# Causal attentions that take two heads at a time, in halves of the tensor engine's array

## The chip, the cores and the metric

The kernel runs on one core of a Trainium2 chip. A core has a tensor engine (PE), which multiplies a stationary operand, loaded into its 128 by 128 array, with a moving one that streams through, and writes to eight PSUM banks of 128 partitions by 512 float32; VectorE (DVE), ScalarE (ACT) and GpSimd (POOL), each with its own queue of instructions; and a DMA queue that SyncE (SP) issues. The metric is the device time of one execution in microseconds, the median of three runs before: 2312.58 us (2312.52 to 2315.58). The profile is that of one further execution.

## The reference

Four layers work on 256 tokens of width 1024 (batch 1), in float32. Layers of the first kind (two) mix four branches, three of which are attentions of 8 heads of width 64; layers of the second kind (two) have one such attention of 4 heads, with width 96 for scores and 64 for values. All four are causal softmax attentions over the 256 tokens:

```python
# fox: decay sums cf of the forget gates enter the scores
logits = jnp.einsum('bqhd,bkhd->bhqk', qb, k).astype(jnp.float32) * scale
logits = logits + cq[..., :, None] - cf[..., None, :]
logits = jnp.where(kpos[None, :] <= qpos[:, None], logits, -jnp.inf)
p = jax.nn.softmax(logits, axis=-1).astype(v.dtype)
return jnp.einsum('bhqk,bkhd->bqhd', p, v)
...
# latent attention, second kind of layer
s = jnp.einsum('bhqd,bhkd->bhqk', q[:, :, start:end], k[:, :, :end]).astype(jnp.float32) * scale
s = jnp.where(qi[:, None] >= ki[None, :], s, -jnp.inf)
p = jax.nn.softmax(s, axis=-1).astype(v.dtype)
outs.append(jnp.einsum('bhqk,bhkd->bhqd', p, v[:, :, :end]))
```

Of moba, whose block is as long as the 256 tokens, plain causal attention is left; dsa masks all but the 64 keys that an index branch scores highest. After the mixer follow gates and projections of the branches, an output product, norms, attention over a memory (second kind) and a feed-forward part.

## The kernel before

**Large products.** Weights stream from memory in chunks of two k tiles by up to 512 columns. ACT rounds a chunk to its high part (`high`, tile `rt<-raw`), DVE subtracts to get the low part (`low`), and PE makes three passes of each product (`mm3`). They are the rows `bank<-rt` of 128x256 or 128x512; 652 chunks of 512 KB feed them, beside some smaller ones. Every other product (`bank<-ft`, plain float32; `bank<-qt`) belongs to the branches.

**Order of the work.** The program is written out once by a planner. It keeps a rough clock of each engine (`Model`, `Engine.cost`) and writes large products one after the other; between them (`tick`) it steps the lanes, generators that write the branches' work piece by piece. A lane's step is written when the planner's clock says that what its last step wrote is done, three PSUM banks are free, and DVE and ACT are not far behind. So the order on each engine is fixed when the program is built; on the chip only semaphores hold an instruction back. The planner prices a float32 product on PE by its stationary and moving widths alone:

```python
one = max(m / 1.2, n / 2.4) + 2
return one if ins[0].dtype == F32R else max(112.0, max(2 * m / 1.2, 4 * n / 2.4))
```

All instructions come from one helper (`call`), so every row of the profile has its line, L362; the tiles tell them apart: `ft` is working memory in float32, `rt` holds rounded operands, `qt` small operands of the decay sums.

**Attention** (`attention`, a lane's generator; lanes A and C in the first kind of layer). One step h does up to three things, for three heads in a software pipeline. Values of head h-2: three products with the transposed probabilities, 128 by 128, as stationary operand and the head's 64 value columns moving. Transposes of head h-1: three of 128 by 128 into a bank, which DVE copies out (`COPY`, 128x384). Scores of head h: q stationary, 64 partitions by 128, against 128 and 256 keys, for fox each after a product that adds the decay sums (`sel`, made by POOL); then DVE adds the mask and takes the minimum (`tensor_tensor_reduce`, the profile's `CUSTOM_DVE_ANT_0`, which is `ISA` in the order), and ACT takes exponentials with their sums. Even heads lie on partitions 0 to 63 and odd ones on 64 to 127. After four heads DVE divides the 128x512 result by the sums, and `attn_out` transposes it (four of 128 by 128) and splits it into high and low part, as the projection needs it. There are 2 x 3 x 8 + 2 x 4 = 56 heads and 14 groups of four.

**Places of other work that the prediction reads.** The index branch of the first kind of layer (`index`) has score products of 64 partitions by 128 and top-8 rounds on DVE. In the second kind of layer the gated branch (`gla`, from L1858) multiplies 32 partitions by 64 columns, in the order that decides what may overlap:

```python
for j in range(2):
    h = 2 * hp + j
    rs = slice(32 * h, 32 * h + 32)
    for q in range(4):
        sl, r = slice(q * 64, (q + 1) * 64), 64 * (q % 2)
        self.mm(bb[j][r:r + 64, q // 2 * 64:q // 2 * 64 + 64], a_[rs, sl], c_[rs, sl])
```

Here `rs` is the row group of the array, `r` its column half (the partitions of the result), and `bb[0]`, `bb[1]` are two banks. The delta branch (`dn`) has products of 128 partitions by 64 columns of 128 moving ones.

Of the kernel before, what the change touches and what calls it, by code (L numbers as in the profile page):

```python
# [14 lines left out]
OP = mybir.AluOpType  # L15
# [44 lines left out]
# branch order in which a mixer's gates and projections are taken  # L60
# [103 lines left out]
class Arena:  # L164
    """Words of a tile, handed out and taken back as the program is written. With aligned set, sizes are
    powers of two and lie at multiples of themselves."""
# [8 lines left out]
    def find(self, free, n):  # L175
        """The offset for n words, or None: the tightest place, the longest unused of these."""
# [95 lines left out]
class Mat:  # L272
    """An operand of the large products in two parts, high and low: [128, a, b] each."""
# [13 lines left out]
class Pair:  # L287
    """Two such operands side by side, of four k tiles each."""
# [16 lines left out]
class Model:  # L305
    """A rough clock of the engines, by which the order of the work is chosen."""
# [45 lines left out]
class Engine:  # L352
    """An engine whose instructions are also put on the model's clock."""
# [37 lines left out]
class Kern:  # L391
    def __init__(self, tc, dram, layers, tiles, due=None):
# [15 lines left out]
        # the stream of weights  # L408
# [87 lines left out]
    def high(self):  # L496
        """High part of the next chunk."""
# [55 lines left out]
    def spawn(self, gen, key=None):  # L553
        """Work in steps that starts now and goes on as its operands come about."""
# [23 lines left out]
    def scoped(self, fn, *args):  # L578
        """Calls fn; returns the time at which all that it wrote is done."""
# [27 lines left out]
    def relieve(self):  # L607
        """Work that may give memory back, ahead of its turn."""
# [22 lines left out]
    def lead(self, name):  # L631
        """How far ahead of its operands a step may be written: nothing where the tensor engine would wait."""
# [25 lines left out]
    def g1(self, out, layer, name, lhs, t, nch, last_use, kt0=0, first=True, last=True, wait=None):  # L658
        """out[token, column] of token tile t over nch chunks of a block; wait(p) sees to the operand of chunk p."""
# [16 lines left out]
    def g11(self, outs, layer, name, lhs, nch, wait):  # L676
        """outs[t][token, column] of both token tiles, chunk by chunk."""
# [14 lines left out]
    def g2(self, outs, layer, name, lhs, cols, nch, last_use=True):  # L692
        """outs[i][channel, token] for column ranges cols of a block."""
# [20 lines left out]
    def head(self, layer, specs, lhs, mid=None):  # L714
        """First blocks after a norm: all of token tile 0, then all of tile 1."""
# [10 lines left out]
    def square_sum(self, f, i, src, eng, scale=1.0):  # L726
        """f[:, i] = sum of squares of scale * src."""
# [7 lines left out]
    def norm_steps(self, t, src, gain, dst, f=None):  # L735
        """Norm of a row tile, into dst() transposed and split; f holds the sums of squares of its halves."""
# [1926 lines left out]
```

## Time and profile before

| what | us |
|---|---|
| median of 3 runs (lowest, highest) | 2312.58 (2312.52, 2315.58) |
| span of the profiled execution | 2314.6 |
| PE busy | 2274.7 (98%) |
| DVE busy | 1509.7 (65%) |
| ACT busy | 1073.3 (46%) |
| POOL busy | 260.7 (11%) |

The profiled execution's own time is its span, 2314.6 us, within the three runs; nothing more of it is given. A busy PE need not be PE at its peak, since matmul spans overlap and their ends are modelled: how long a group of passes takes is read from its start to the start of what follows. The clock that PE was granted is full (1.00) in the mixers of the first kind of layer.

### The profile page before, as it was taken

The page shows a single profiled execution, that of the slowest core. Times are in us where ns is not written, and L with a number is a line of the kernel's source. Part 1 is how long each engine was busy: PE and PEld are TensorE (multiplying, and loading weights), DVE is VectorE, ACT ScalarE, POOL GpSimd, SP SyncE. Part 2 cuts the span into 40 slices and gives each one's busy share as a digit, 9 for nine tenths or more (in the row PEclk, how much of TensorE's full clock was granted, in tenths as well). Part 3 has the DMA queues.
Part 4 walks back from the last instruction along what each step waited for, and adds up shares of the span by engine and source line. Part 5 has one row for each costly group of instructions (what it writes and reads, how often), then busy time and mean ns, then how long its engine had stood idle before and what let it go on. Part 6 is the DMA issues. An engine that isn't in the chain of part 4 may idle for free.

```text
span 2314.6 us, 40370 instructions
## 1 busy us (share of the span) xinstructions
PE 2274.7 (98%) x16412; PEld 2060.1 (89%) x16412; DVE 1509.7 (65%) x2397; ACT 1073.3 (46%) x1691; POOL 260.7 (11%) x244
## 2 busy tenths in 40 slices
PE   8999999999999999999999999999999999999998
PEld 6888998899788899889988899988988889998897
DVE  7777657555877655765578767555556786755554
ACT  4454445444445544544454335444445424544543
POOL 3012020000300302000021320000002132000000
PEclk9999999999999999999999999999999999999999
DMA  6434556655533345565544336456553424645563
GB/s 224 140 116 136 149 180 207 199 173 167 175 126 126 124 157 196 177 234 190 168 128 139 100 119 216 149 172 226 182 165 126 150 84 136 216 146 168 190 202 109
DMA packets 106662, 375.48 MB, mean 162 GB/s; under 512 B 12474, under 2 KB 12908, under 8 KB 106476
## 3 DMA queue, kind: packets, MB, share of 16 engines
q1 hardware_dynamic: 106476, 372.91, 49.3%
q8 instruction: 128, 2.10, 0.4%
q14 instruction: 58, 0.48, 0.1%
HBM read 371.81 MB, written 1.05 MB: 161 GB/s over the span
## 4 chain that ended last, share of the span: by engine, by line
PE 89%; DVE 5%; issue 2%; DMA 1%; ACT 1%; POOL 1%; SPq 0%; POOLq 0%; DVEq 0%; ACTq 0%
PE bank L362 89%; DVE ft L362 3%; DVE rt L362 2%; DMA raw<-in_wts_a 1%; POOL ft L362 1%; ACT rt L362 1%; DMA ft<-in_positions 0%; ACT ft L362 0%; SPq L430 0%; ACT junk L362 0%; DVE junk L362 0%; POOLq L2658 0%; DVEq L362 0%; POOLq L362 0%; ACTq L362 0%
## 5 line engine op out<-in xcount | busy, mean ns | idle before, releaser
L362 PE MATMUL bank<-rt 128*128 128x256 f32 (+2 forms) x12720 | 2001.7, 316 | 13.9 <-DVE rt L362 13.8
L362 PEld LDWEIGHTS bank<-rt 128*128 128x128 f32 x12720 | 1778.7, 191 | 175.1 <-DVE rt L362 19.3
L362 DVE TENSOR_TENSOR rt<-raw,rt 128x1024 fp32r<-128x1024 f32 (+2 forms) x692 | 838.7, 1238 | 343.1 <-ACT rt L362 341.7
L362 ACT ACTIVATE rt<-raw 128x1024 fp32r<-128x1024 f32 (+2 forms) x692 | 698.3, 1034 | 381.2 <-PE bank L362 216.3
L362 POOL TENSOR_TENSOR ft<-ft 128x512 f32<-128x512 f32 (+7 forms) x186 | 211.7, 1146 | 1826.1 <-DVE ft L362 1593.4
L362 PE MATMUL bank<-ft 64*64 64x64 f32 (+10 forms) x3644 | 361.2, 263 | 19.1 <-DVE ft L362 12.3
L362 PEld LDWEIGHTS bank<-ft 128*128 128x128 f32 (+6 forms) x3644 | 288.9, 154 | 67.8 <-DVE ft L362 15.7
L362 ACT ACTIVATE ft<-bank 128x512 f32<-128x512 f32 (+4 forms) x252 | 133.6, 535 | 312.9 <-PE bank L362 274.5
L362 ACT ACTIVATE ft<-ft 128x128 f32<-128x128 f32 (+7 forms) x206 | 88.6, 440 | 229.3 <-DVE ft L362 218.0
L362 DVE SCALAR_TENSOR_TENSOR ft<-ft 128x512 f32<-128x512 f32 (+5 forms) x211 | 94.0, 467 | 41.9 <-ACT junk L362 20.6
L362 DVE TENSOR_TENSOR ft<-ft 128x512 f32<-128x512 f32 (+5 forms) x122 | 69.2, 568 | 65.9 <-ACT ft L362 62.9
L362 DVE SCALAR_TENSOR_TENSOR ft<-bank,ft 128x254 f32<-128x254 f32 (+6 forms) x176 | 80.5, 482 | 31.8 <-ACT ft L362 12.8
L362 ACT ACTIVATE rt<-bank 128x512 fp32r<-128x512 f32 (+1 forms) x102 | 56.0, 554 | 96.2 <-PE bank L362 95.3
L362 DVE TENSOR_TENSOR ft<-ft,bank 64x512 f32<-64x512 f32 (+3 forms) x92 | 59.4, 645 | 36.7 <-PE bank L362 30.3
L362 ACT ACTIVATE ft<-bank,ft 128x256 f32<-128x256 f32 x108 | 47.3, 482 | 72.8 <-PE bank L362 49.9
L362 DVE TENSOR_TENSOR ft<-bank,ft 128x512 f32<-128x512 f32 (+7 forms) x138 | 59.9, 468 | 29.2 <-PE bank L362 18.3
L362 DVE SCALAR_TENSOR_TENSOR ft<-ft,bank 128x512 f32<-128x512 f32 (+1 forms) x106 | 67.4, 642 | 17.0 <-PE bank L362 9.9
L362 DVE COPY ft<-bank 128x384 f32<-128x384 f32 (+6 forms) x96 | 51.9, 543 | 39.7 <-PE bank L362 37.8
L362 ACT ACTIVATE rt<-ft 128x512 fp32r<-128x512 f32 x58 | 36.5, 630 | 60.5 <-DVE ft L362 60.5
L362 POOL TENSOR_SCALAR qt<-qt,ft 64x256 fp32r<-64x256 f32 (+1 forms) x32 | 33.0, 1033 | 190.9 <-PE bank L362 190.7
L362 ACT ACTIVATE junk<-ft 128x512 bf16<-128x512 f32 (+1 forms) x46 | 27.2, 590 | 58.8 <-DVE ft L362 56.2
L362 DVE SCALAR_TENSOR_TENSOR rt<-bank,rt 128x512 fp32r<-128x512 f32 (+1 forms) x72 | 43.4, 612 | 14.3 <-ACT rt L362 14.2
(37 smaller groups left out, 308.3 us busy)
## 6 DMA issues: line engine op xcount, KB each, us to landing
raw<-in_wts_a SPq DMA_DIRECT2D x340, 512.0 KB, 4.3
raw<-in_wts_b SPq DMA_DIRECT2D x312, 512.0 KB, 4.3
raw<-in_wts_b SPq DMA_DIRECT2D x24, 256.0 KB, 2.7
raw<-in_wts_b SPq DMA_DIRECT2D x8, 440.0 KB, 4.2
raw<-in_wts_a SPq DMA_DIRECT2D x8, 340.0 KB, 4.6
ft<-in_mem SPq DMA_DIRECT2D x4, 512.0 KB, 8.2
ft<-in_x SPq DMA_DIRECT2D x2, 512.0 KB, 3.3
ft<-in_norm_mix_pre SPq DMA_DIRECT2D x2, 512.0 KB, 5.5
```

Of the source, the lines that this page charges most:

```text
L362: r = None if self.dry else f(*args, **kw)
```

## The change

`attention` takes two heads (a pair) in each step. Scores: the four products of both heads (eight for fox) are written alternately, even head on the upper 64 rows of the array, odd head on the lower, into two banks. Softmax: the exponentials' sums are inverted at once, four numbers a pair, and DVE multiplies each head's probabilities (128 and 256 columns) ahead of their transposes. Values: the head's 64 value columns are stationary and the transposed probabilities move (256 columns for the first keys, 128 for the second); even heads write to partitions 0 to 63 of the result and odd ones to 64 to 127, so the result comes out transposed. `attn_out` only splits it, from the bank, or from a copy that ACT makes where there is no room yet for the split result. `sel` makes the decay operands of both heads.

```diff
     def attention(self, heads, qk, sel, bias, v, dst, done):
...
+        st, extras = {}, {}
+        ybank, held = None, []
...
+        n = heads // 2
+        tiles = ((0, 128), (128, 384))
+        room = lambda: self.R.fits(128 * heads, 128 * heads)
...
-        for h in range(heads + 2):
...
-                self.mm(yb[:, 0, hh % 4], pt.a[:, 0:128], v(0, hh))
-                self.mm(yb[:, 1, hh % 4], pt.a[:, 128:256], v(0, hh), stop=False)
-                self.mm(yb[:, 1, hh % 4], pt.a[:, 256:384], v(1, hh), start=False)
...
+        for i in range(n + 2):
+            if i >= 2:
+                pr = i - 2
+                pts = st.pop(("pt", pr))
+                if pr % 2 == 0:
+                    ybank = self.bank()
+                o = 256 * (pr % 2)
+                for kt in range(2):
+                    for j, pt in enumerate(pts):
+                        rows = slice(64 * j, 64 * j + 64)
+                        if kt == 0:
+                            self.mm(ybank[rows, o:o + 256], v(0, 2 * pr + j), pt.a[:, 0:256], stop=False)
+                        else:
+                            self.mm(ybank[rows, o + 128:o + 256], v(1, 2 * pr + j), pt.a[:, 256:384], start=False)
+                for pt in pts:
+                    pt.free()
+            if 1 <= i <= n:
+                ps, pts = st.pop(("p", i - 1)), []
+                for p in ps:
+                    b = self.bank()
+                    for c in range(3):
+                        self.tr(b[:, 128 * c:128 * c + 128], p.a[:, 128 * c:128 * c + 128])
+                    pt = F.alloc(384, "pt")
+                    self.copy(pt.a, b[:, :384])
+                    self.fbank(b)
+                    p.free()
+                    pts.append(pt)
+                st[("pt", i - 1)] = pts
+            if i < n:
+                qks = [qk(2 * i + j) for j in range(2)]
+                bb = [self.bank() for _ in range(2)]
+                extra = extras.pop(i) if sel else None
+                if sel and i + 1 < n:
+                    extras[i + 1] = sel(i + 1)
+                for t in range(2):
+                    sl = slice(128 * t, 128 * t + 128)
...
+                        for j in range(2):
+                            f, rr = extra[0][j]
+                            self.mm(bb[j][:, 256 * t:256 * t + 256], f[:, sl], rr, stop=False)
+                    for j in range(2):
+                        q, k = qks[j]
+                        self.mm(bb[j][:, 256 * t:384 * t + 128], q[:, sl], k[:, 0:128 * t + 128], start=extra is None)
...
-                             accum=rsv[:, i, h:h + 1])
+                    extra[1].free()
+                ps, nm = [F.alloc(384, "p") for _ in range(2)], F.alloc(16, "nm")
+                nv = nm.v(4, 2, 2)
+                for j in range(2):
+                    for t, (a, c) in enumerate(tiles):
+                        self.V.tensor_tensor_reduce(out=ps[j].a[:, a:c], in0=bb[j][:, 2 * a:2 * a + c - a], in1=bias[:, a:c],
+                                                    scale=1.0, scalar=3e38, op0=OP.add, op1=OP.min,
+                                                    accum_out=nv[:, 0, j, t:t + 1])
+                    self.fbank(bb[j])
+                    for t, (a, c) in enumerate(tiles):
+                        self.act(ps[j].a[:, a:c], ps[j].a[:, a:c], AF.Exp, scale=-1.0, bias=nv[:, 0, j, t:t + 1],
+                                 accum=nv[:, 1, j, t:t + 1])
+                self.V.reciprocal(nm.a[:, 8:12], nm.a[:, 4:8])
+                for j in range(2):
+                    for t, (a, c) in enumerate(tiles):
+                        self.ts(ps[j].a[:, a:c], ps[j].a[:, a:c], nv[:, 2, j, t:t + 1], OP.mult)
...
-                self.V.reciprocal(ri.v(2, 4), rsv[:, :, 4 * g:4 * g + 4])
-                self.tt(y.v(8, 64), view(ybank[0], 8, 64), ri.a[:, :, None].to_broadcast([128, 8, 64]), OP.mult)
...
+                st[("p", i)] = ps
+            if i >= 2 and pr % 2 == 1:
+                y, yb, ybank = None, ybank, None
+                if not (m or room()):
+                    y = F.alloc(512, "y")
+                    self.act(y.a, yb)
+                    self.fbank(yb)
+                    held.append((y, pr // 2))
+                else:
+                    m = m or Mat(self, heads // 2, 256, "yT")
+                    self.spawn(self.attn_out(m, None, yb, pr // 2), key)
+            elif held and (m or room()):
...
+                for y, g in held:
+                    self.spawn(self.attn_out(m, y, y.a, g), key)
+                held = []
+            yield
+        while not m and not room():
...
+        for y, g in held:
+            self.spawn(self.attn_out(m, y, y.a, g), key)
...
-    def attn_out(self, m, y, g):
...
-                self.tr(b[:, 256 * c + 128 * t:256 * c + 128 * t + 128], yv[:, t, c])
...
+    def attn_out(self, m, y, src, g):
+        yield from self.split(m, (slice(None), slice(2 * g, 2 * g + 2), slice(None)), view(src, 2, 256))
+        if y is None:
+            self.fbank(src)
+        else:
+            y.free()
...
-            def sel(h):
-                r = slice(64 * (h % 2), 64 * (h % 2) + 64)
-                f = lsel(8 + h, r, 256)
-                return f.a[r], st["rr"].a[r], f
+            def sel(i):
+                f, ops = self.Q.alloc(256, "lsel"), []
+                for j in range(2):
+                    r = slice(64 * j, 64 * j + 64)
+                    c = 8 + 2 * i + j
+                    self.ts(f.a[r], f32(st["base"].a)[r], self.sel[r, c:c + 1], OP.mult, eng=self.P)
+                    ops.append((f.a[r], st["rr"].a[r]))
+                return ops, f
```

On PE, fox in the first layer: a step of before holds values (`128x64 x3`), transposes and scores of one head each (`qt` and `ft` into one bank), then large products (`rt`).

```order
L362 MATMUL bank_74<-ft 128x64 x3
L362 MATMUL bank_68<-ft 128x128 x3
L362 MATMUL bank_70<-qt 128x256
L362 MATMUL bank_70<-ft 128x128
L362 MATMUL bank_70<-qt 128x256
L362 MATMUL bank_70<-ft 128x256
L362 MATMUL bank_75<-rt 128x256 x30
```

And a step of after, at the same place of the program.

```order
L362 MATMUL bank_71<-ft 64x256 x2
L362 MATMUL bank_71<-ft 64x128 x2
L362 MATMUL bank_72<-ft 128x128 x3
L362 MATMUL bank_73<-ft 128x128 x3
L362 MATMUL bank_69<-qt 128x256
L362 MATMUL bank_68<-qt 128x256
L362 MATMUL bank_69<-ft 128x128
L362 MATMUL bank_68<-ft 128x128
L362 MATMUL bank_69<-qt 128x256
L362 MATMUL bank_68<-qt 128x256
L362 MATMUL bank_69<-ft 128x256
L362 MATMUL bank_68<-ft 128x256
```

A step now has the values of two heads (partitions 64, rows `64x256` and `64x128`), six transposes, and scores that alternate between two banks; the large products behind it are not shown.

On DVE, moba in the first layer: of before, the copy of transposes, the two reductions of a head with the reads of their results, and, once in four heads, the reciprocal and the division of the result.

```order
L362 COPY ft<-bank_70 128x384
L362 ISA ft<-bank_69,ft 128x128
L362 ISA ft 128x1
L362 ISA ft<-bank_69,ft 128x256
L362 ISA ft 128x1
L362 RECIPROCAL ft<-ft 128x8
L362 TENSOR_TENSOR ft<-bank_72,ft 128x512
L362 MAX ft<-ft 128x8
```

And of after, from the reductions of a pair's second head on.

```order
L362 ISA ft<-bank_70,ft 128x128
L362 ISA ft 128x1
L362 ISA ft<-bank_70,ft 128x256
L362 ISA ft 128x1
L362 RECIPROCAL ft<-ft 128x4
L362 TENSOR_SCALAR ft<-ft 128x128
L362 TENSOR_SCALAR ft<-ft 128x256
L362 TENSOR_SCALAR ft<-ft 128x128
L362 TENSOR_SCALAR ft<-ft 128x256
L362 TENSOR_TENSOR rt<-raw,rt 128x1024 x2
L362 MAX ft<-ft 128x8
```

The reciprocal now stands in each pair directly behind the reductions, with the four multiplications; weight halves (`rt<-raw`) and the index branch come behind them.

## Rows read from the trace of the kernel before

**Rows 1.** The page's head and its busy line.
```profile
span 2314.6 us, 40370 instructions
...
PE 2274.7 (98%) x16412; PEld 2060.1 (89%) x16412; DVE 1509.7 (65%) x2397; ACT 1073.3 (46%) x1691; POOL 260.7 (11%) x244
```
**Rows 2.** The chain of waits: start, length, engine and tile.
```profile
37.03 349.70 PE bank L362 x2424
...
615.78 342.81 PE bank L362 x2395
```
**Rows 3.** Busy time by engine, sum of 55:115, 115:180 and 180:285.
```profile
sum 230.00, PE 230.00 PEld 203.28 DVE 160.62 ACT 113.42 POOL 26.67; mean PE 76.67 PEld 67.76 DVE 53.54 ACT 37.81 POOL 8.89
```
**Rows 4.** Groups by shape, DVE, 55:285: busy us, mean ns | idle before, releaser.
```profile
L362 DVE TENSOR_TENSOR rt<-raw,rt 128x1024 fp32r<-128x1024 f32 x60 | 75.5, 1273 | 12.0 <-ACT rt L362 12.0
...
L362 DVE CUSTOM_DVE_ANT_0 ft<-bank,ft 128x128 f32<-128x128 f32 x24 | 6.9, 289 | 12.0 <-PE bank L362 11.9
```
**Rows 5.** Who PE waited for: us in total, times, longest.
```profile
PE bank L362 <- DVE rt L362: 13.8, 16, 2.8
PE bank L362 <- DVE ft L362: 12.3, 6, 7.6
```
**Rows 6.** Timeline of a moba head, PE and its loads: start us, us, instruction.
```profile
88.36 1.96 PE L362 MATMUL bank<-ft 128*128 128x64 f32 x13
89.40 0.52 PEld L362 LDWEIGHTS bank<-ft 64*128 64x128 f32 x4 [0.17 <-issue]
90.25 2.94 PEld L362 LDWEIGHTS bank<-rt 128*128 128x128 f32 x24 [0.33 <-issue]
```
**Rows 7.** Timeline of a fox head, and of a step without scores, PE.
```profile
145.36 1.11 PE L362 MATMUL bank<-ft 128*128 128x64 f32 x9
146.39 0.38 PE L362 MATMUL bank<-qt 64*128 64x256 f32 x1
...
147.48 0.74 PE L362 MATMUL bank<-rt 128*128 128x256 f32 x4
...
164.92 1.11 PE L362 MATMUL bank<-ft 128*128 128x64 f32 x9
165.79 2.31 PE L362 MATMUL bank<-rt 128*128 128x512 f32 x9
```
**Rows 8.** Timeline of passes in half of the array, PE (index, delta branch).
```profile
50.02 0.71 PE L362 MATMUL bank<-ft 64*128 64x128 f32 x4
...
58.34 1.13 PE L362 MATMUL bank<-ft 64*128 64x256 f32 x4
...
1360.03 0.65 PE L362 MATMUL bank<-ft 128*64 128x128 f32 x4
1360.61 0.62 PE L362 MATMUL bank<-rt 128*128 128x256 f32 x3
```
**Rows 9.** Timeline of products in quarters and eighths, PE (gated branch).
```profile
1331.06 0.47 PE L362 MATMUL bank<-ft 32*64 32x64 f32 x16
1331.46 0.74 PE L362 MATMUL bank<-rt 128*128 128x256 f32 x4
```
**Rows 10.** Groups by shape, DVE, the whole span: multiplications by a column.
```profile
L362 DVE TENSOR_SCALAR ft<-ft 128x256 f32<-128x256 f32 x30 | 10.5, 371 | 2.3 <-ACT ft L362 1.7
...
L362 DVE TENSOR_SCALAR ft<-ft 128x128 f32<-128x128 f32 x3 | 0.8, 267 | 2.5 <-ACT ft L362 2.4
```
**Rows 11.** Timeline behind the scores of the moba head above, DVE and ACT.
```profile
90.47 0.29 DVE L362 CUSTOM_DVE_ANT_0 ft<-bank,ft 128x128 f32<-128x128 f32 x1 [0.40 <-PE bank L362]
...
90.80 0.40 ACT L362 ACTIVATE ft<-ft 128x128 f32<-128x128 f32 x1 [3.27 <-DVE ft L362]
91.03 0.08 DVE L362 DVE_READ_ACCUMULATOR2_ANT ft<- 128x1 f32 x1
...
91.84 0.20 DVE L362 RECIPROCAL ft<-ft 128x8 f32<-128x8 f32 x1 [0.73 <-ACT ft L362]
92.08 0.69 DVE L362 TENSOR_TENSOR ft<-bank,ft 128x512 f32<-128x512 f32 x1
```

More of the change, by code (lines that the diff above doesn't have):

```diff
@@ L861, in attention @@
         m = None
-        rs = F.alloc(2 * heads + 8, "rs")
-        rsv = rs.v(2, heads)
-        st = {}
-        ybank, ydone, held = [None], None, []
+        st, extras = {}, {}
+        ybank, held = None, []
         key = ("y", id(dst))
-        extras = {}
+        n = heads // 2
+        tiles = ((0, 128), (128, 384))
+        room = lambda: self.R.fits(128 * heads, 128 * heads)
         if sel:
@@ L870, in attention @@
             yield
-        for h in range(heads + 2):
-            if h >= 2:
-                hh = h - 2
-                pt = st.pop(("pt", hh))
-                if hh % 4 == 0:
-                    ybank[0] = self.bank()
-                yb = view(ybank[0], 2, 4, 64)
-                self.mm(yb[:, 0, hh % 4], pt.a[:, 0:128], v(0, hh))
-                self.mm(yb[:, 1, hh % 4], pt.a[:, 128:256], v(0, hh), stop=False)
-                self.mm(yb[:, 1, hh % 4], pt.a[:, 256:384], v(1, hh), start=False)
-                pt.free()
-            if 1 <= h <= heads:
-                p = st.pop(("p", h - 1))
-                b = self.bank()
-                for i in range(3):
-                    self.tr(b[:, 128 * i:128 * i + 128], p.a[:, 128 * i:128 * i + 128])
-                pt = F.alloc(384, "pt")
-                self.copy(pt.a, b[:, :384])
-                self.fbank(b)
-                p.free()
-                st[("pt", h - 1)] = pt
-            if h < heads:
-                q, k = qk(h)
-                b = self.bank()
-                extra = extras.pop(h) if sel else None
-                if sel and h + 1 < heads:
-                    extras[h + 1] = sel(h + 1)
-                for i in range(2):
-                    sl = slice(128 * i, 128 * i + 128)
-                    if extra:
-                        self.mm(b[:, 256 * i:256 * i + 256], extra[0][:, sl], extra[1], stop=False)
-                    self.mm(b[:, 256 * i:384 * i + 128], q[:, sl], k[:, 0:128 * i + 128], start=extra is None)
-                if extra:
-                    extra[2].free()
-                p = F.alloc(384, "p")
-                nm = F.alloc(8, "nm")
-                for i, (a, c) in enumerate(((0, 128), (128, 384))):
-                    self.V.tensor_tensor_reduce(out=p.a[:, a:c], in0=b[:, 2 * a:2 * a + c - a], in1=bias[:, a:c],
-                                                scale=1.0, scalar=3e38, op0=OP.add, op1=OP.min, accum_out=nm.a[:, i:i + 1])
-                self.fbank(b)
-                for i, (a, c) in enumerate(((0, 128), (128, 384))):
-                    self.act(p.a[:, a:c], p.a[:, a:c], AF.Exp, scale=-1.0, bias=nm.a[:, i:i + 1],
-                             accum=rsv[:, i, h:h + 1])
-                nm.free()
-                st[("p", h)] = p
-            if h >= 2 and (h - 2) % 4 == 3:
-                g = (h - 2) // 4
-                ri = F.alloc(8, "ri")
-                y = F.alloc(512, "y")
-                self.V.reciprocal(ri.v(2, 4), rsv[:, :, 4 * g:4 * g + 4])
-                self.tt(y.v(8, 64), view(ybank[0], 8, 64), ri.a[:, :, None].to_broadcast([128, 8, 64]), OP.mult)
-                self.fbank(ybank[0])
-                ri.free()
-                if ydone:
-                    held.append(ydone)
-                ydone = (y, g)
-            elif h >= 2 and ydone and (m or self.R.fits(128 * heads, 128 * heads)):
@@ L928, in attention @@
                 m = m or Mat(self, heads // 2, 256, "yT")
-                self.spawn(self.attn_out(m, *ydone), key)
-                ydone = None
+                for y, g in held:
+                    self.spawn(self.attn_out(m, y, y.a, g), key)
+                held = []
             yield
-        rs.free()
-        while not m and not self.R.fits(128 * heads, 128 * heads):
+        while not m and not room():
             yield
         m = m or Mat(self, heads // 2, 256, "yT")
-        for a in held + [ydone]:
-            self.spawn(self.attn_out(m, *a), key)
+        for y, g in held:
+            self.spawn(self.attn_out(m, y, y.a, g), key)
@@ L941, in attention @@
         done()
-    def attn_out(self, m, y, g):
-        b = self.bank()
-        yv = y.v(2, 2, 128)
-        for c in range(2):
-            for t in range(2):
-                self.tr(b[:, 256 * c + 128 * t:256 * c + 128 * t + 128], yv[:, t, c])
-        yield from self.split(m, (slice(None), slice(2 * g, 2 * g + 2), slice(None)), view(b, 2, 256))
-        self.fbank(b)
-        y.free()
+    def attn_out(self, m, y, src, g):
[4 more added lines that the diff above has]
+            y.free()
     def rope(self, b, nh, t, dup=False):
```

## The prediction

> **What bounds the kernel now.** I read the busy shares first: the tensor engine (PE) stands at 98%, VectorE (DVE) at 65%, ScalarE (ACT) at 46% [rows 1]. A busy PE is not yet a bound, since matmul spans overlap, so the chain of waits comes next: one piece of it is 349.70 us of PE without a break, from 37 to 387 us, which is the whole mixer of the first layer with its three attentions; the second layer has its like [rows 2]. In such a stretch time taken from PE is time taken from the span, until another engine is late. The next view is therefore what DVE does there: in 55 to 285 us, where the 24 heads of layer one lie, it is busy 160.6 of 230 us [rows 3], and its idle time is mostly the time in which it stands ahead of PE: 12.0 us for ACT's half of the next weight chunk and 12.0 us before the first read of the scores are the largest pieces [rows 4]. PE waits for DVE 13.8 + 12.3 us in the whole program [rows 5]. So PE bounds, and DVE has about 69 us to give per layer of the first kind.
>
> **Prices on PE.** A product of float32 operands runs as two passes, each a row of the trace. One moba head: the step starts at 88.36, its scores at 89.40 (the first weight load of 64 rows), the large products go on at 90.25; so 1.04 us for values and transposes and 0.85 us for scores [rows 6]. A fox head takes 1.03 and 1.09 us [rows 7]. The step at 164.92, which has no scores, takes 0.87 us for 6 value passes and 3 transposes, 0.097 us each; with scores behind them the same nine take 0.16 to 0.17 us more, which is the way into 64 rows [rows 6, 7]. In half of the array, four passes of 256 columns take 1.13 us and four of 128 take 0.71, so 128 columns cost 0.105 us and 256 cost 0.21; four of 128 columns in a column half take 0.58 us to the next large product, 0.16 over 4 x 0.105, which is the switch in and out [rows 8].
>
> Do halves run beside each other? The row that bears on it is a score step of the gated branch: 16 passes of 32 rows by 64 columns, which alternate between column halves and go from one row group to the next with the head, end after 0.40 us [rows 9]. A 64-column pass is half of 0.105, so 0.052 us. One after the other they would take 16 x 0.052 + 0.16 = 1.0 us, two at a time 0.58, four at a time 0.37. Measured is 0.40: both row groups and column halves overlap. What no row shows is the width that is used here, 64 rows by 128 columns and 128 rows by 64 with 256 moving; I take the same.
>
> [...]
>
> **The change, part by part (PE).**
> Values: before, 6 passes a head at 0.097, so 1.16 us for two heads. Now 4 passes of 256 and 4 of 128, two at a time: 2 x 0.21 + 2 x 0.105 = 0.63, plus 0.16 for the switch and up to 0.17 for the way in: 0.96. Saved 0.20 us a pair, 28 pairs: 5.6 us.
> Scores: before, each head pays its own stay in 64 rows, 0.85 + 0.17 = 1.02 us (moba, dsa), 1.09 + 0.16 = 1.25 (fox). Now two heads share one stay, in two banks. Saved 1.02 x 16 pairs + 1.25 x 8 pairs = 16.3 + 10.0 = 26.3 us. The four pairs of latent attention have 96 rows and save nothing here.
> Transposes of probabilities: as many as before. Transposes of the result: 4 for each of 14 groups go, 56 x 0.097 = 5.4 us.
> Sum 5.6 + 26.3 + 5.4 = 37 us of PE.
>
> **The change on the other engines.** DVE gains four multiplications a pair, 2 x (0.371 + 0.267) = 1.28 us [rows 10], and a reciprocal of 0.20 [rows 11]. That reciprocal stands right behind the four reductions of both heads and waits for the last exponential, with all of DVE's queue behind it: weight halves, copies for the next step, convolutions. Where a reciprocal now follows one head's exponentials it waited 0.73 us. For two heads: ACT starts 0.33 us after the first reduction and needs 1.04 a head (90.80 to 91.84), so 2.41 us; DVE is busy with reductions for 2 x 0.64 = 1.28 of it (90.47 to 91.11 a head); the wait is 1.1 us [rows 11]. What goes is the division of the result per group, 0.69 + 0.20 + 0.73 = 1.6 us, 0.8 a pair. Net 1.28 + 0.20 + 1.1 - 0.8 = 1.8 us a pair: 21 us in the 12 pairs of a layer, 50 us in all. Layer one's DVE then has 160.6 + 21 = 182 us of queue in 230 - 18 = 212 us of PE (the 18 being half of 37), 86%. So most of it lies in idle time; ACT gains only four copies of a result that finds no room yet, and POOL's work for fox is the same.
> Bounds of what DVE takes back: 0, if the idle time takes all; 50 us, if every pair pays all on the path. The planner (which prices a product in half the array as if it ran alone, and reciprocals and multiplications below their rows) places the next step by its own clock, and between two moba steps stand 48 to 54 large passes, some 6 us, against a chain of reductions, exponentials and multiplications of 1.3 + 1.1 + 1.5 = 3.9 us behind the scores. That fits with 2 us to spare, less whatever stands in DVE's queue ahead. Nearest is the row in which PE waits for DVE only 26 us in the whole program while DVE is idle 69 in one mixer, so I take a fifth, 10 us.
> The rest of the program is planned anew behind each of these steps; PE's waits for DVE there, 26.1 us [rows 5], can move by a few us either way.
>
> **Sum.** The profiled execution had a span of 2314.6 us [rows 1], 2.0 above the median 2312.6 of the three runs, so nothing measurable lies around it. 2314.6 - 37 + 10 = 2287.6 by the span, 2286 by the median. Likeliest case by itself: 2275 (DVE takes nothing back) to 2296 (20 us, twice what I take).
>
> **Rivals.**
> DVE becomes the bound in the mixers (slower than before at its end). Place: the reciprocal behind the exponentials. For it: 86% in a queue that is kept in order, and moba shares its stretch with the top-8 rounds of the index branch. Against: DVE stands ahead of PE in the rows above. With half of the 50 us on the path: 2312.6 - 37 + 25 = 2301. With all of it: 2326. It decides from 37 / 28 = 1.3 us a pair.
> [...]
> Row halves take turns, since each pass fills all 128 output partitions. Of the 26.3 us then stays one way in per pair, 24 x 0.17 = 4: 2286 + 22 = 2308, no change that can be told.
> DVE takes nothing, and in the new order a quarter of the 26.1 us that PE waits for DVE goes too: 2275.6 - 6.5 = 2269.
>
> **How the numbers follow.** About 0.2% (4.6 us) is what a measurement of this kernel can tell from no change. Forecast 2286 (2275 to 2296): 0.62. DVE with half, 2301: 0.12. DVE with all or more, 2317 and above: 0.06. Column halves in turn, 2304: 0.07. Row halves in turn, 2308: 0.05. Below 2275: 0.08. The range that leaves out two in ten: 2267 to 2306. Faster (under 2308): the forecast, the lower case, half DVE and columns, 0.89; within 0.2%: 0.05; slower: 0.06.
>
> **What would show it.** Values right: in each pair 8 rows of 128 x 64 with starts in twos, some 0.8 us to the first transpose; in turn, 1.4. Scores right: the first score to the next large product about 0.9 us for two moba heads and 1.1 for two fox heads; 1.6 or more if rows take turns. DVE right: reciprocals of 4 columns x28 with about 1.1 us idle before each, put down to ACT, and 70% busy turned into some 80% in the mixers; PE's waits for DVE up by about 10 us. The forecast is wrong if large products in 55 to 285 us show gaps before the transposes that wait for DVE by more than 1.3 us a pair, or if the mixer's unbroken PE piece does not shorten by 13 to 18 us.

## The result, and the profile after

The changed kernel takes 2298.95 us (median of 4 runs, 2296.01 to 2300.51), the kernel before 2312.55 us (4 runs on the same chip, 2308.87 to 2315.58). The ratio is 0.9938, its 95% interval 0.9922 to 0.9953: 13.6 us faster, about half of the 26 us forecast. The profiled execution is the fastest of the four runs, and that of before, a further one, is slower than all four of its kernel (a run's time is 1.8 us above its span wherever both are given, which makes it about 2316.4), so the two traces differ by more than the medians: 2314.6 - 2294.2 = 20.4 us of span.

The page of the changed kernel, its head and its busy line:

```profile
span 2294.2 us, 40097 instructions
...
PE 2237.2 (98%) x16244; PEld 2020.1 (88%) x16244; DVE 1526.5 (67%) x2509; ACT 1074.2 (47%) x1695; POOL 271.2 (12%) x244
```

PE still reads 98%, as before [rows 1]: that number hides the loss. The chain of waits shows it in the second layer, whose mixer was one piece of 342.81 us [rows 2] and now lies in several, the longest of them:

```profile
609.01 48.96 PE bank L362 x326
...
695.62 35.68 PE bank L362 x227
...
742.26 59.18 PE bank L362 x377
...
806.12 141.63 PE bank L362 x1092
```

Of the first layer's mixer it shows nothing: followed back from its end, this chain reaches only to 587 us. What ends PE's waits:

```profile
PE bank L362 <- DVE rt L362: 27.7, 20, 3.1
PE bank L362 <- DVE ft L362: 12.0, 6, 7.4
...
PE bank L362 <- POOL qt L362: 3.4, 2, 1.7
```

The wait for `rt` from DVE, which is the low halves of weights, has doubled from 13.8 us [rows 5]; the wait for `ft` is as it was; the one for `qt`, an operand of the state branch made on POOL, is new. The three windows of the first layer's heads, engines in the order PE, PEld, DVE, ACT, POOL, then granted clock, busy share of DMA and GB/s:

```profile
55.00:115.00 60.00, 60.00 (x418) 50.80 (x418) 46.83 (x135) 31.61 (x66) 7.92 (x5) 1.00 0.44 141
115.00:180.00 65.00, 60.16 (x380) 50.56 (x379) 56.53 (x120) 32.86 (x67) 9.56 (x7) 0.95 0.44 137
180.00:285.00 105.00, 101.89 (x755) 92.86 (x754) 67.34 (x132) 50.52 (x98) 17.38 (x13) 1.00 0.46 145
sum 230.00, PE 222.05 PEld 194.22 DVE 170.70 ACT 114.98 POOL 34.86; mean PE 74.02 PEld 64.74 DVE 56.90 ACT 38.33 POOL 11.62
```

PE was busy 230.00 of 230 [rows 3]; now 8 us of the stretch are idle, while DVE stands at 74%. DVE is not full, and PE waits for it: the average does not say what stands ahead of what. The first of the layer's three holes, in a timeline of DVE and PE (start, length, instruction):

```profile
121.92 1.39 DVE L362 TENSOR_TENSOR rt<-raw,rt 128x1024 fp32r<-128x1024 f32 x1
...
121.96 3.86 PE L362 MATMUL bank<-rt 128*128 128x256 f32 x30
123.23 1.01 DVE L362 COPY ft<-bank 128x384 f32<-128x384 f32 x2
...
124.17 0.28 DVE L362 CUSTOM_DVE_ANT_0 ft<-bank,ft 128x128 f32<-128x128 f32 x1
...
126.44 0.18 DVE L362 RECIPROCAL ft<-ft 128x4 f32<-128x4 f32 x1 [1.09 <-ACT ft L362]
126.66 1.01 DVE L362 TENSOR_SCALAR ft<-ft 128x128 f32<-128x128 f32 x4
...
127.58 2.36 DVE L362 TENSOR_TENSOR rt<-raw,rt 128x1024 fp32r<-128x1024 f32 x2
...
128.85 2.36 PE L362 MATMUL bank<-rt 128*128 128x256 f32 x10 [3.03 <-DVE rt L362]
```

A low half ends at 123.3; the next starts at 127.58, 4.3 us later, behind two copies, the four reductions, 1.09 us of waiting, a reciprocal and four multiplications, and takes 1.2. PE's products last until 125.8, 2.5 us from 123.3. It is 4.3 + 1.2 - 2.5 = 3.0 us short, and that is its wait, 3.03. What follows the hole (same columns as the windows above):

```profile
126.00:129.00 3.00, 0.15 (x1) 0.15 (x2) 2.52 (x7) 2.78 (x6) 0.00 (x0) 1.00 0.09 34
129.00:131.00 2.00, 1.88 (x10) 1.64 (x11) 1.93 (x4) 0.00 (x0) 0.00 (x0) 0.66 0.56 109
131.00:133.00 2.00, 2.00 (x11) 1.78 (x12) 1.93 (x5) 0.00 (x0) 0.00 (x0) 0.50 0.93 356
133.00:135.00 2.00, 2.00 (x22) 1.51 (x24) 1.89 (x5) 0.00 (x0) 0.00 (x0) 0.98 0.17 68
```

The granted clock falls to 0.66 and 0.50 in the two windows after the hole, which costs 2 x 0.34 + 2 x 0.50 = 1.7 us more. (That is an estimate: it takes PE's work to go with the clock.) The other two holes of the layer end here:

```profile
176.46 0.38 PE L362 MATMUL bank<-qt 32*128 32x256 f32 x1 [1.68 <-POOL qt L362]
...
240.25 0.98 PE L362 MATMUL bank<-rt 128*128 128x256 f32 x6 [3.11 <-DVE rt L362]
```

The third is of the first one's kind, a wait for a low half. The second is not: there PE waits 1.68 us for `qt` from POOL, and the clock falls too (0.64 from 176.40 to 180.00). The sister layer has the same three, 3.04, 1.70 and 3.10 us.

### The profile page after: what moved, and what is told of

The parts are those of the page before. It is cut to its first block, busy times and chain, and to the rows that moved or that the text cites. A ratio compares the mean times of both kernels' runs of the same rounds, so it can differ in the third digit from the quotient of the medians.

```text
span 2294.2 us, 40097 instructions
## 1 busy us (share of the span) xinstructions
PE 2237.2 (98%) x16244; PEld 2020.1 (88%) x16244; DVE 1526.5 (67%) x2509; ACT 1074.2 (47%) x1695; POOL 271.2 (12%) x244
## 4 chain that ended last, share of the span: by engine, by line
PE 63%; DVE 6%; issue 2%; ACT 1%; DMA 1%; POOL 1%; SPq 0%; POOLq 0%; DVEq 0%; ACTq 0%
PE bank L362 63%; DVE ft L362 4%; DVE rt L362 2%; POOL ft L362 1%; ACT rt L362 1%; ACT ft L362 0%; DMA raw<-in_wts_a 0%; DMA raw<-in_wts_b 0%; DMA ft<-in_positions 0%; POOL qt L362 0%; ACT junk L362 0%; SPq L430 0%; DVE junk L362 0%; POOLq L2676 0%; DVEq L362 0%
## 5 line engine op out<-in xcount | busy, mean ns | idle before, releaser
L362 PE MATMUL bank<-rt 128*128 128x256 f32 (+2 forms) x12720 | 1993.5, 316 | 28.0 <-DVE rt L362 27.7
L362 PE MATMUL bank<-ft 64*64 64x64 f32 (+11 forms) x3476 | 315.6, 266 | 18.8 <-DVE ft L362 12.0
L362 PEld LDWEIGHTS bank<-ft 64*64 64x64 f32 (+6 forms) x3476 | 243.7, 147 | 74.5 <-issue 16.0
L362 ACT ACTIVATE ft<-bank 128x512 f32<-128x512 f32 (+5 forms) x256 | 135.7, 536 | 317.6 <-PE bank L362 290.2
L362 DVE TENSOR_SCALAR ft<-ft 128x256 f32<-128x256 f32 (+7 forms) x236 | 55.4, 277 | 21.3 <-ACT ft L362 9.8
L362 DVE TENSOR_TENSOR ft<-bank,ft 128x512 f32<-128x512 f32 (+8 forms) x124 | 50.3, 442 | 16.1 <-PE bank L362 7.5
L362 POOL TENSOR_SCALAR qt<-qt,ft 64x256 fp32r<-64x256 f32 (+1 forms) x32 | 42.1, 1318 | 131.4 <-PE bank L362 130.5
L362 ACT ACTIVATE junk<-ft 128x512 bf16<-128x512 f32 (+1 forms) x46 | 27.2, 591 | 58.1 <-DVE ft L362 55.6
```

Of the source, the lines that this page charges most:

```text
L362: r = None if self.dry else f(*args, **kw)
```

## A view that the experiments need

All kernels here run the same 12720 large products in the same order. So the start of the n-th of them in each trace, against before, says where time comes and goes; a median only gives the sum. Differences in us, worked out from the traces; positions are behind the attentions of the mixers (first kind, first kind, second, second) and the end:

```
large product        1920    5040    7680   10800   12719
before, us          364.2   915.9  1391.4  1970.5  2307.1
after                -7.4   -10.6   -16.7   -20.1   -20.1
e1 no division      -18.9   -36.5   -37.9   -40.0   -40.1
e2 no mult.         -16.0   -33.1   -29.3   -22.6   -22.6
e3 own step         -16.0   -33.2   -25.9   -23.8   -23.7
e4 price             +1.3    +0.2    +5.4   +18.1   +18.1
e5 own step, first  -18.3   -35.4   -40.3   -39.3   -39.2
e8 plan of after    -13.1   -25.4   -34.3   -37.6   -37.6
e11 latent only      +2.5    +2.5    -2.4    -5.6    -5.6
e12 low earlier     -11.7   -25.5   -31.3   -32.4   -32.2
```

Counted from the span's start, the rows come out up to 0.5 us lower. Up to 2.5 us of a row (3.9 in e12) are there already at product 200, ahead of the first heads. Behind 5040 a row also holds the granted clock of two single executions, and that differs between executions of one kernel: of the runs of before beside e5, one of 2308.23 us had a mean of 0.997 and one of 2318.01 us had 0.992. In the trace of before the clock is 1.00 up to product 5280; its mean is 0.981 from there to 7680 and 0.988 from 7680 to 10800.

## The experiments

Each stood beside runs of before on the same chip; ratios are against those.

**e1: no division.**
```diff
-                self.V.reciprocal(nm.a[:, 8:12], nm.a[:, 4:8])
-                for j in range(2):
-                    for t, (a, c) in enumerate(tiles):
-                        self.ts(..., nv[:, 2, j, t:t + 1], OP.mult)
```


> Leaves out the reciprocals and the multiplications of the probabilities, so the result is not divided; all products stay as in the changed kernel. In the changed kernel the tensor engine's branch products take 34 us less than before, and its large products 14 us more, most of it in gaps of 3 us in which it waits for the low halves of weights. Theory A (the block of reciprocal, its wait of 1.1 us and 1.0 us of multiplications stands in VectorE's queue between two low halves): the gaps go, 14 us come back, 2285 us. Theory B (the gaps come from where the planner puts the low halves, whatever stands in the queue): within 4 us of the changed kernel, 2295 to 2303.

2273.08 us, 0.9825 (0.9812 to 0.9838): 26 us under the changed kernel, where theory A had 14. Theory B's time is out as well, but this run can't separate the two, since without the division the planner also chooses other places (e8 can). In the first two mixers e1 is 18.9 and 36.5 us ahead of before: the whole saving on PE that the prediction worked out for them, 18 us each. The 26 us between e1 and after there (36.5 - 10.6) are the price of the division.

**e2: the multiplications left out, the reciprocal kept.**
```diff
                 self.V.reciprocal(nm.a[:, 8:12], nm.a[:, 4:8])
-                for j in range(2): ...   # the four multiplications
```


> Keeps the reciprocal and its wait for the exponentials, leaves out the four multiplications (the result is not divided). If the wait in the queue costs (1.2 of the block's 2.3 us with the reciprocal itself), half of what leaving out all gives: about 2292 us. If the multiplications as work cost, nearly all of it: 2286. If neither: 2295 to 2303.

2295.1 us, 0.9922 (0.9909 to 0.9936). The median alone would say that the multiplications cost 4 us. The table says otherwise: in the first two mixers e2 is 33.1 us ahead, 22.5 us better than after; the second kind's mixers then lose 10.5 us, where after gained 9.5, with a new order of their own in which the missing multiplications, of 4 latent pairs, can't cost anything. With 1 us less in each block most holes close (up to product 5040 PE waits 12.4 us, 26.1 in after), although the reciprocals wait as before (30.0 us in all). So neither the wait nor the work has a price of its own here. What fits is that their sum uses up a small stock of low halves, which e12 tests.

**e3: reciprocal and multiplications as a step of their own.**
```diff
+                yield
                 self.V.reciprocal(nm.a[:, 8:12], nm.a[:, 4:8])
```


> The reciprocal and the multiplications become a step of their own, which the planner writes when the exponentials are done by its clock; the work is the same. If the wait of 1.1 us in VectorE's queue is what makes low halves late: the idle time before the reciprocals falls from 30.3 us in all to under 10 and the time to about 2290 us. If the work costs and not the wait: the idle time falls too, the time stays at 2295 to 2303. If probabilities come later to their transposes by this: slower, 2305.

2292.66 us, 0.991 (0.9897 to 0.9924). The reciprocals' idle time falls from 30.3 us to nothing, and the first two mixers get 22.6 of the 25.9 us back (33.2 against 10.6), with all the work still there. Again the second kind loses, 9.4 us, by 10800.

**e4: the planner's price of half-array products halved.**
```diff
-            return one if ... else max(112.0, max(2 * m / 1.2, 4 * n / 2.4))
+            return one if ... else self.part * max(112.0, max(2 * m / 1.2, 4 * n / 2.4))
```
(`self.part` is 0.5 around the values, and around scores of 64 rows.)

> Only the planner's price changes: the products of values and scores that run two at a time are priced at half. By its own clock a fox pair takes 3.0 us for values and scores where the trace has 2.0 with the transposes' share taken off, so it believes the tensor engine to be later than it is and writes low halves late. If that makes the gaps: two or more of the six gaps of 3 us go, and the time falls to 2286 to 2292 us. If the order of the queue alone makes them: 2295 to 2303.

2334.19 us, 1.0088 (1.0072 to 1.0103): slower than before, by 21 us. My sign was wrong. The planner writes a low half that is not due yet when DVE's clock is no more than 1500 ns ahead of PE's; a PE clock that runs late lets it write low halves early. The truer price takes that cover away:

```profile
PE bank L363 <- DVE rt L363: 34.4, 30, 4.0
PE bank L363 <- DVE ft L363: 22.9, 15, 7.3
```

PE waits 34.4 us for low halves instead of 27.7 and 22.9 us for `ft` instead of 12.0, and the whole gain of the first two mixers is gone (+0.2 at 5040). These 17.6 us are less than half of the 38.2 by which the span is longer than that of after, and the loss goes on in the second kind (+18.1 at 10800), so the lost cover is the likely cause, argued and not shown; that the price alone moves the time the wrong way is measured.

**e5: e3 in the first kind alone.**
```diff
+                if qks[0][0].shape[0] == 64:
+                    yield
                 self.V.reciprocal(nm.a[:, 8:12], nm.a[:, 4:8])
```


> The reciprocal and the multiplications are a step of their own in the two layers of the first kind alone; the latent attentions of the second kind keep them behind the reductions. With the step of its own everywhere, the first kind's two mixers came 33 us earlier at the same large product than in the kernel before, and the second kind's mixers lost 9 us; the changed kernel's second kind won 10. If the first is due to the step and the second to a new order in layers where the step brings nothing, both gains now add: 2313 - 33 - 10 = 2270 us, 2266 to 2280 with what the new order may do. If the second kind's loss follows from the state in which the first kind leaves the queues: 2290 to 2295 again.

2276.88 us, 0.9836 (0.9816 to 0.9856), with the division whole: it beats both kernels, the changed one by about 22 us. The place of the hole above, in e5:

```profile
120.28 7.94 PE L362 MATMUL bank<-rt 128*128 128x256 f32 x64
120.40 1.01 DVE L362 COPY ft<-bank 128x384 f32<-128x384 f32 x2
121.33 0.28 DVE L362 CUSTOM_DVE_ANT_0 ft<-bank,ft 128x128 f32<-128x128 f32 x1
...
122.44 0.08 DVE L362 DVE_READ_ACCUMULATOR2_ANT ft<- 128x1 f32 x1
122.44 1.22 DVE L362 TENSOR_TENSOR rt<-raw,rt 128x1024 fp32r<-128x1024 f32 x1
```

The low half stands right behind the last reduction, in the time in which DVE used to wait for the exponentials. PE runs 64 products instead of 30 and a hole. The windows' sum over the same 230 us:

```profile
sum 230.00, PE 229.31 PEld 202.38 DVE 178.89 ACT 121.82 POOL 35.38; mean PE 76.44 PEld 67.46 DVE 59.63 ACT 40.61 POOL 11.79
```

DVE is busier than in the changed kernel (178.89 against 170.70 us) and PE is full again. The two gains did not add as expected: the second kind gives 3.8 us here (35.4 to 39.2), not 10; the time came out within the range because the first kind gave 35.4 and not 33.

**e6 and e7: one head's passes written behind the other's,** from e1, the planner's clock fed as before (the edit in outline).
```diff
-                for t in range(2):
-                    for j in range(2):
+                for j in range(2):
+                    for t in range(2):
```
(e6 in the scores; e7 the same with `kt` in the values.)

> From the kernel without reciprocals and multiplications (2273 us, the tensor engine bound): the scores of one head are written behind those of the other instead of in turns, with the planner's clock fed as before, so that nothing else changes its place. The result is not divided. If the two row halves work beside each other, and only where passes of both are next to each other: 16 pairs lose 0.5 us and 8 pairs 0.9 us, less one pass of overlap each, 8 to 15 us: 2281 to 2288. If the gain came from the shared stay in 64 rows alone: within 3 us of 2273.

> The same with the values: both products of one head are written before those of the other; the scores stay in turns. The result is not divided. If the column halves work beside each other: a pair's passes cost up to 4 x 0.21 + 4 x 0.105 instead of half of it, 0.63 us less the overlap of one pass, 28 pairs, 12 to 18 us: 2285 to 2291. If they take turns anyway: 2273.

2276.52 us (0.9831, 0.9811 to 0.9851) and 2272.38 us (0.9816, 0.9798 to 0.9834): neither differs from e1 by what can be told. They did not decide what they were meant to, since for values and for the scores of moba and dsa the written order is not the order of the starts. In e6 the passes of two heads still start 13 ns apart, and two moba heads' scores take 0.86 us (65.96 to 66.82), as in e1 (65.98 to 66.84). In e7 a pair's eight passes still start in twos, 13 and 14 ns apart (7 ns in e1), the four of 256 columns ahead of the four of 128, and take what they took, 94.83 to 95.63:

```profile
94.83 0.88 PE L465 MATMUL bank<-ft 128*64 128x256 f32 x8
95.63 1.57 PE L362 MATMUL bank<-rt 128*128 128x256 f32 x11
```

For fox the order did count. There six passes of one head stand ahead of six of the other, and a pair's scores take 1.42 us in e6 (111.19 to 112.62) instead of 1.09 in e1 (111.19 to 112.28), in all eight pairs, 2.7 us in sum:

```profile
111.19 0.38 PE L465 MATMUL bank<-qt 64*128 64x256 f32 x1
...
112.62 2.66 PE L362 MATMUL bank<-rt 128*128 128x256 f32 x20
```
```profile
111.19 0.39 PE L362 MATMUL bank<-qt 64*128 64x256 f32 x2
...
112.28 2.90 PE L362 MATMUL bank<-rt 128*128 128x256 f32 x22
```

**e8: e1 with the order of the changed kernel** (the edit in outline).
```diff
+                dry, self.V.dry = self.V.dry, True    # counted by the planner, not issued
                 self.V.reciprocal(...)                # and the four multiplications
+                self.V.dry = dry
```


> The changed kernel with its own plan, word for word the same order on all engines, but the reciprocals and multiplications are left out of VectorE's queue (the planner's clock still counts them; the result is not divided). Leaving them out of the plan too gave 2273 us. If the block in the queue makes the low halves late: the six gaps of 1.9 to 3.3 us in the first kind's mixers go and the time is 2270 to 2280. If the planner's places make them: the gaps stay, 2293 to 2301.

2280.69 us, 0.9853 (0.9829 to 0.9878). With every other instruction in its place 14.8 of the 25.9 us come back in the first two mixers (25.4 against 10.6); the other 11 are places that the planner chose because it counts the division, such as the wait for `qt`, which stays at 1.69 us. So queue and plan share the price, in these traces about four to three up to product 5040; at the end e8 and e1 differ by only 2.5 us.

**e9 and e10: both heads in one half of the array,** from e1 with its plan (in outline; fox's decay operands go with the scores, and e10 also writes one head behind the other, which cost nothing in e7).
```diff
-                        q, k = qks[j]
+                        q, k = qks[0] if heads == 8 else qks[j]
```
```diff
-                        rows = slice(64 * j, 64 * j + 64)
+                        rows = slice(0, 64)
```


> From the kernel without reciprocals and multiplications (2273 us), with its plan: the scores of a pair are both computed from the first head's operands, so all passes lie in the same 64 rows; number, size, banks and order stay. What is computed for the second head of a pair is wrong. Writing the heads behind one another cost nothing (2276.5 +- 3), and in its trace the passes of the two heads still start 13 ns apart, so the order doesn't decide; the place does. If row halves work beside each other: 16 pairs lose 0.52 us (2 x 0.21 + 2 x 0.105 less the overlap) and 8 pairs about 0.95, in all 15 to 18 us: 2288 to 2291. If halves are no help: 2273.

> From the same kernel, with its plan: the values of both heads of a pair go through the same 64 columns (into the same rows of the result, so half of it is lost). If column halves work beside each other: 28 x 0.63 = 17.6 us more, 2288 to 2292. If they took turns before too: 2273.

2289.91 us (0.9887, 0.9872 to 0.9903) and 2290.13 us (0.9894, 0.9881 to 0.9908): 16.8 and 17.1 us over e1, as expected. (e1 ran on another chip; by the ratios it is 14 and 16 us, and PE's branch products, idle time taken off, take 16.9 and 17.9 us more in the traces.) A pair's values in one half, and a moba pair's scores in one half:

```profile
98.63 1.51 PE L465 MATMUL bank<-ft 128*64 128x256 f32 x8
100.07 10.20 PE L362 MATMUL bank<-rt 128*128 128x256 f32 x52
```
```profile
66.89 1.57 PE L465 MATMUL bank<-ft 64*128 64x128 f32 x8
68.39 4.58 PE L362 MATMUL bank<-rt 128*128 128x256 f32 x36
```

And the same two in e1:

```profile
65.98 0.93 PE L362 MATMUL bank<-ft 64*128 64x128 f32 x8
66.84 4.58 PE L362 MATMUL bank<-rt 128*128 128x256 f32 x36
...
95.01 0.87 PE L362 MATMUL bank<-ft 128*64 128x256 f32 x8
95.81 6.75 PE L362 MATMUL bank<-rt 128*128 128x256 f32 x37
```

1.44 us instead of 0.80 for the values, 1.50 instead of 0.86 for the scores, and 1.97 instead of 1.09 for fox. So in e1 both kinds of halves work beside each other.

**e11: the latent attentions alone** (in outline).
```diff
-            yield from self.attention(4, ...)     # kernel before
+            yield from self.attention2(4, ...)    # the changed function, here alone
```


> The kernel before, with the change in the four latent pairs of the second kind alone. On the tensor engine these save 0.2 + 0.2 us a pair, 1.6 us in all. In the changed kernel the two second-kind mixers came 9.6 us earlier than before at the same large product. If that is the change's own effect there: 2313 - 10 = 2303, 2301 to 2306. If it came from the state in which the mixers of the first kind leave queues and plan, or from chance in the new order: another number, anywhere from 2305 to 2320.

2309.35 us, 0.9976 (0.9967 to 0.9985): 5.2 us by the median, 8.1 in the trace from 5040 to the end (+2.5 to -5.6). So the change is worth something in these layers by itself, about 5 us, more than the 1.6 of PE work. The larger number of the traces is in part the granted clock: between products 5280 and 10800 it takes 15.3 us from before, 10.2 from e11 and 8.5 from after (what is missing to 1.00, summed), which is 5.1 of e11's 8.1 us and 6.8 of the 9.5 of after (10.6 to 20.1). PE's waits do not explain it: behind product 5280 they are 17.0 us in e11 and 17.4 before. In e2 and e3 they are 27.2 and 28.6, so the next order may lose as much.

**e12: low halves earlier.**
```diff
+        if self.chunks[min(self.i_cur, len(self.chunks) - 1)][0][0] == "a":
+            idle += 1500.0
```


> The changed kernel; in the layers of the first kind the planner may write a low half when VectorE's clock is up to 3000 instead of 1500 ns ahead of the tensor engine's. The work is the same. If the gaps come from too few low halves in stock when the block of a pair stands in the queue: the gaps of 3.2 us go, 14 to 25 us come back: 2274 to 2285. If the stock cannot grow (buffers, or the high halves of ACT): 2295 to 2303. If earlier low halves push scores' reductions back: slower than 2303.

2283.82 us, 0.9867 (0.9853 to 0.988), 15 us under the changed kernel with the same work. The reciprocals still wait (30.0 us), and 14.9 of the 25.9 us come back in the first two mixers. The same allowance holds for ACT's high halves, which may come earlier too. Halves in stock cover the block, as the step of its own moves it; e4 acts on the same condition, the other way round.

## Why the prediction was right in sign and half wrong in size

**PE's saving: right.** 37 us worked out; from each branch product's start to the next start the traces add up to 322.3 us before and 288.1 after, 34.2 less; with PE's idle time taken off they are 313.1 and 275.0, 38.1 less. A pair's values take 0.80 us (0.8 foreseen), two moba heads' scores 0.86 (0.9), two fox heads' 1.09 (1.1):

```profile
134.54 0.39 PE L362 MATMUL bank<-qt 64*128 64x256 f32 x2
134.76 0.38 PE L362 MATMUL bank<-ft 64*128 64x128 f32 x4
134.90 0.37 PE L362 MATMUL bank<-qt 64*128 64x256 f32 x2
135.11 0.60 PE L362 MATMUL bank<-ft 64*128 64x256 f32 x4
135.63 1.58 PE L362 MATMUL bank<-rt 128*128 128x256 f32 x11
```

Taking the halves from each other costs 17 us each (e9, e10), so it is out that halves take turns, in rows or in columns. In e1 both heads' values fill all 128 rows (`128*64`), and their overlap is worth 17 us (e10). No run shows the 2304 us that the forecast's chances have for column halves in turn; what e10 shows is 17.1 us over e1 with a pair's values in one column half.

**DVE's block: right in size.** A reciprocal waits 30.3 / 28 = 1.08 us (1.1 foreseen) and takes 0.18; the four multiplications take 1.01 us (1.28 foreseen; the four rows overlap by 0.1 us each):

```profile
L362 DVE RECIPROCAL ft<-ft 128x4 f32<-128x4 f32 x28 | 5.0, 178 | 30.3 <-ACT ft L362 30.3
```

**What DVE takes back: mis-sized.** The failed step is "I take a fifth, 10 us", with its ground, that the chain behind the scores "fits with 2 us to spare". That chain did fit: PE's waits for `ft` from DVE are 12.0 us, as before. What was late was the other work that the text had named as queued behind the reciprocal and then left out of the sum: the low halves, in two of a layer's three holes (the one for `qt`, 1.7 us, was not thought of). Their cover is not DVE's idle share of a mixer, 69 us, but the products in stock at that moment, 2.5 us of them in the hole above. The price in the first two mixers was 26 us, where 24 of the 28 pairs, and so 8.6 of the 10 us, were placed. By size it is the rival with half of the 50 us (2301), though DVE never filled: it stood at 74%, where the forecast had some 80. The measured 2298.95 us lies outside the forecast's own case (2275 to 2296), next to that rival, and inside the wider range alone. The forecast's own mark said so too: the mixers had to shorten by 13 to 18 us, and did by 7.4 and 4.0 (the second from -6.8 us at product 3480 to -10.8 at 5280, counted from the span's start).

**The clock: not foreseen.** Part of the 26 us is PE running at a lower granted clock after a hole, by the estimate above 1.7 us after the first, and (1 - 0.64) x 3.6 + (1 - 0.91) x 5 = 1.8 us after the second. Holes of 7.8 us and these 3.5 make 11.3, against 11.5 us between after and e1 at product 1920. In the second layer the clock fell after all three holes (0.64 from 695.62 to 698, 0.51 from 744 to 746, 0.50 from 806.12 to 812.12): 0.978 on the mean of the 307 us from product 3480 to 5280, which is 6.8 us. Up to product 5040 PE waits 26.1 us in after and 9.6 in e1, where the clock is 1.00: 16.5 us of waits and 3.5 + 6.8 of clock make 26.8, against the price of 25.9.

```profile
176.40:180.00 3.60, 3.54 (x10) 2.74 (x11) 2.69 (x6) 2.09 (x3) 2.61 (x4) 0.64 0.76 270
180.00:185.00 5.00, 5.00 (x26) 4.11 (x25) 1.38 (x3) 0.94 (x3) 1.10 (x1) 0.91 0.38 116
```

**The second kind: not foreseen.** 9.5 us came in its mixers in the traces, where the sum had 1.6; 6.8 of them are the clock of the two executions (e11). In all, 36.5 - 25.9 + 9.5 = 20.1 us in the traces. The medians have 13.6, so some 3 us are left for the second kind, if the 10.6 up to product 5040 hold in other executions too. A gain that the sum did not have is luck as far as the forecast goes; it covers a small part of what DVE's term lacked, 26 - 8.6 = 17 us. (The execution that the sum starts from was, as a run's time, not 2.0 but about 3.8 us above the median; the differences in the sum stay.)

## What to carry to other kernels

The reciprocals, which waited 1.08 us each in DVE's queue, were paid by the low halves behind them (holes of 3.03 and 3.11 us on PE). So price an instruction that waits against the stock of the work that stands behind it at that place, not against the engine's idle share; then write other work into the wait (e5) or stock up ahead of it (e12). When a planner orders the program, compare traces at equal progress of the bounding engine before believing a median: e2's and e3's medians hide 22 us of gain under another layer's loss. Compare the granted clock of the two executions as well, or it passes for a gain (6.8 of 9.5 us in the second kind here). A planner's wrong price can be what makes it work: correcting it alone cost 35 us against the changed kernel (e4). No run here corrects the price together with the slack.

## What the runs showed of the hardware that was not expected

Passes in different halves of the array started in twos even where the program writes four of one half ahead of four of the other (e6, e7: 13 to 14 ns apart, against 6 to 7 in the changed kernel, where the same are written in turns). With six ahead of six, fox's scores in e6, they did so in part, and the pair took 1.42 us instead of 1.09. Whether the engine or a translation below the program does it, no run here shows. Two holes cost more than half of their length again through the granted clock, by the estimate above (1.7 us after one of 3.03, 1.8 after one of 1.68), and one did not: after the hole at 237, 3.11 us long, the clock stayed at 1.00. The same hole in the sister layer, 3.10 us up to 806.12, was followed by 6 us at 0.50.

```profile
237.00:240.20 3.20, 0.14 (x2) 0.00 (x0) 2.32 (x6) 3.15 (x10) 0.00 (x0) 1.00 0.05 20
240.20:243.00 2.80, 2.75 (x23) 2.30 (x24) 0.45 (x1) 1.97 (x5) 0.00 (x0) 1.00 0.58 173
```
